# One hybrid-attention layer on one core: the compressed branch's bias table by DMA, its last logits by two products, and transpositions that begin with the selected branch

## The chip, the cores and the metric

The kernel runs on one core of a Trainium2 chip. The core has a matrix engine (TensorE, PE in the rows, with PEld for its weight loads), VectorE (DVE), ScalarE (ACT), GpSimd (POOL) and SyncE (SP), each with an instruction queue of its own that is worked in order. DMAs are started from SP's and POOL's queues, a few from ACT's. The metric is the device time of one execution in microseconds (us), the median of the runs shown.

## The reference

One layer, sequence 512, width 2048, everything in float32:

```
h  = x @ W_in                              (2048 x 11808: q, k, v, gates, z of both attentions)
yA = (FoX(qA, kA, vA, f) * silu(zA)) @ W_A      8 heads of 128, forget-gate bias
yB = (NSA(qB, K/V per branch, gates) * silu(zB)) @ W_B   8 heads, 2 key/value groups
x  = LayerNorm(alpha * x + (sigmoid(gA) * yA + sigmoid(gB) * yB) @ W_o)
```

NSA adds three branches per head, each with its own softmax and its own gate:

```
compressed: 31 blocks of 32 tokens, stride 16; keys/values from a small MLP over each block
            logits = q . k_cmp / sqrt(128) + rel_bias[bucket(t - block_end)], masked where block_end > t
selected:   8 of 8 blocks of 64 tokens at this length, that is causal attention over all 512
window:     the last 512 tokens, causal
every logit gets rel_bias[bucket(distance)] of its head (32 buckets)
```

## The kernel before, in words

Every product of the reference is made in float32 accuracy from split operands: `split` writes a value's rounded part (hi) with ACT and the rest (lo) with DVE, and `mm3` (L106) adds hi x hi, hi x lo and lo x hi into one PSUM bank. A weight tile of 128x512 takes one ACT operation (wh) and one DVE operation (wl) before TensorE can use it.

The program is one long stream of *units*, each of some 12 or more dense products on one weight chunk. Chunks come by SP's queue into three buffers (wr), the splits run three units ahead. Within a unit a *step* of the background work (`tick`) follows every two k-tiles, that is every six dense products. A step advances the generators in `active` and `copies`, then one step of the queue of transposition jobs, then one of the queue of logits jobs. So the order of the instructions on every engine is written out by this program; nothing is decided on the chip, and each engine waits on semaphores in that order.

The stages: first the transposition of x and the first projections, in which `tables` builds the bias tables; then projections by a seven-product scheme with sums on DVE and accumulating DMAs from POOL's queue; the eight FoX heads (about 560 to 840 us), the compression MLP among them (`cmp_units`, `cmp_finish`); the eight NSA heads (about 840 to 1120 us); the outputs.

The bias of the compressed branch: `tables` writes the bias by distance into a row of DRAM (rel_d), `spread` writes it 31 times to DRAM (fwd_d), and in FoX `block_bias` fetches for each head a tile cbT [31 blocks x 512 tokens], whose four 128-token pieces TensorE transposes (L706) into a pt bank, and DVE copies them into cb [128 tokens, head, row tile, 32 blocks]. `nsa_s` adds cb to the compressed logits (L544).

An NSA head has two jobs. `nsa_s` (logits) makes eight items in eight steps: row tiles 0 to 2 of the selected branch together with the compressed one ("sc"), the compressed logits of row tile 3 alone ("c", three products of 32 columns), the selected row tile 3, then three of the window branch. Each item goes through a product, a row minimum and exponential one step later, and a scaling by 1/sum and gate another step later. At step n = 7 the compressed weights are normalised into tc3. `nsa_t` (transpositions and values) waits for the whole of that, then transposes tc3 (L599), the four column tiles of the selected weights p (L417) and those of the window, splits each on ACT and DVE (pT), and three steps after its transposition multiplies it with the values into one bank o. There are two pt banks, two s banks for logits, and one o bank.

Of the kernel before, what the change touches and what calls it, by code (L numbers as in the profile page):

```python
# [40 lines left out]
NEG = -1e30  # L41
SC = DH ** -0.5
RL = 640
FL = 1023
OFF = [P * i * (i + 1) // 2 for i in range(NT)]
PW = P * NT * (NT + 1) // 2
FIRST = 16512
# [16 lines left out]
def layer(ctx, tc, x, w_in, b_f, pos_k, pos_v, wk1, wk2, wv1, wv2, w_a, w_b, w_o, ln_g, ln_b, rel, onehot, out):  # L64
# [446 lines left out]
    def nsa_s(h, st):  # L511
        key, g = ("n", h), h // HPG
        yield from wait_for(("q", key), ("k", ("s", g)), ("k", ("w", g)))
        bt = pool("nsa").tile([P, S], F32, name="bt", tag="bt", bufs=2)
        nc.gpsimd.dma_start(bt, dram(skew_d, h * P * RL + P - 1, [[RL - 1, P], [1, S]]))
        yield
        st["s"], st["st"] = yield from take_p()
        st["w"], st["wt"] = yield from take_p()
        q, k = qt[key], kt_[g]
        tcm = pool("nsa").tile([P, NT, CP], F32, name="tc", tag="tc", bufs=1)  # L520

        def mm(it):
            i, br = it["i"], it["br"]
            n = (i + 1) * P
            t0 = slice(i * P, (i + 1) * P)
            b = bank("s", 2)
            it["bias"] = bt[:, (NT - 1 - i) * P:]
            if i == 0:
                def both(u):
                    return k[:, u, :2 * S].rearrange("p (b c) -> p b c", b=2)[:, :, :CP + P]  # L530
                mm3(b[:, :2 * (CP + P)].rearrange("p (b c) -> p b c", b=2), (q[:, 0, t0], q[:, 1, t0]),
                    (both(0), both(1)), True, True)
                it["b"], it["logits"] = b, b[:, CP:CP + P]
                it["other"].update(logits=b[:, 2 * CP + P:2 * (CP + P)], bias=it["bias"])
                return
            c0 = {"c": 0, "sc": 0, "s": CP, "w": CP + S}[br]
            nn = {"c": CP, "sc": CP + n, "s": n, "w": n}[br]
            mm3(b[:, :nn], (q[:, 0, t0], q[:, 1, t0]), (k[:, 0, c0:c0 + nn], k[:, 1, c0:c0 + nn]), True, True)
            it["b"] = b
            it["logits"] = b[:, CP:CP + n] if br == "sc" else b[:, :n]  # L540

        def red(it):
            if it["br"] in ("c", "sc"):
                nc.vector.tensor_tensor(tcm[:, it["i"]], it["b"][:, :CP], cb[:, h, it["i"]], op=ALU.add)  # L544
            if it["br"] != "c":
                exp_row(it)
# [13 lines left out]

        steps = items("s", 1, [(0, "sc"), (1, "sc"), (2, "sc"), (3, "c"), (3, "s")])
        other = items("w", 2, [(i, "w") for i in range(NT)])
        steps[0]["other"] = other[0]
        steps += other[1:]
        mc, lc, rc = stat("mn"), stat("l"), stat("r")
        for n, _ in enumerate(staged(steps, (mm, red, norm))):
            if n == 5:
                nc.vector.tensor_reduce(mc, tcm, axis=AX.X, op=ALU.max)
                nc.vector.tensor_tensor(tcm, tcm, mc[:, :, None].to_broadcast([P, NT, CP]), op=ALU.subtract)
                nc.scalar.activation(tcm, tcm, AF.Exp)  # L570
            if n == 7:
                nc.vector.tensor_reduce(lc, tcm, axis=AX.X, op=ALU.add)
                nc.vector.reciprocal(rc, lc)
                nc.vector.tensor_tensor(rc, rc, gates[:, :, 3 * h], op=ALU.mult)
                yield from take_later("tc")

                st["c"] = tc3 = pool("nsa").tile([P, NT, C3], F32, name="tc3", tag="tc3", bufs=1)
                nc.vector.tensor_tensor(tc3.rearrange("p i (u c) -> p i u c", u=3),
                                        tcm[:, :, None, :].to_broadcast([P, NT, 3, CP]),
                                        rc[:, :, None, None].to_broadcast([P, NT, 3, CP]), op=ALU.mult)  # L580
            if n == 7:
                done.add(("s", key))
                free["q"] += 1
            yield
        done.add(("p", key))

    def nsa_t(h, st):
        key, g = ("n", h), h // HPG
        yield from wait_for(("p", key), ("v", ("s", g)), ("v", ("w", g)))
        yield from take_later("o")  # L590
        o = bank("o", 1)

        def tr(it):
            if "p" in it:
                tr_p(it)
                return
            it["b"] = b = bank("pt", 2)
            for i in range(NT):
                nc.tensor.transpose(b[:C3, i * P:(i + 1) * P], st["c"][:, i], ident)  # L599
            free["tc"] += 1  # L600

        def spl(it):
            if "p" in it:
                split_p(it)
                return
            it["t"] = t = pt_tile()
            src, c, low = it.pop("b")[:C3], t[:C3, 0], slice(CP, 2 * CP)
            nc.scalar.activation(c, src, AF.Copy)
            nc.vector.tensor_tensor(c[low], src[low], c[low].bitcast(F32), op=ALU.subtract)

        def prod(it):
            if "p" in it:
                pv(it)
                return
            nc.tensor.matmul(o, vt["c", g], it.pop("t")[:C3, 0], start=True, stop=False)

        def items(nm):
            return [dict(j=j, p=st[nm], tag=st[nm + "t"], v=vt[nm, g], o=o, first=False, last=nm == "w" and j == NT - 1)
                    for j in range(NT)]

        yield from staged([{}] + items("s") + items("w"), (tr, spl, None, prod))
        gate_out(key, H + h, o)
        done.add(("t", key))

# [8 lines left out]
        return pool("hd").tile([P, S], F32R, name=name, tag="om", bufs=KT)[:p, :n]  # L633


    rel_d = dp.tile([H, RL + FL], F32, name="rel_d")
    skew_t = dp.tile([H, P, RL], F32, name="skew_d")
    skew_d = skew_t[:]
    fwd_t = dp.tile([H, NCMP, FL], F32, name="fwd_d")
    fwd_d = fwd_t[:]  # L640
    negc_t = dp.tile([H, S], F32, name="negc_d")
    negc_d = negc_t[:]
    zd = [dp.tile([P, S], F32, name=f"z_d{h}") for h in range(NZD)]
# [6 lines left out]
    def tables():  # L650
# [3 lines left out]
        nc.gpsimd.dma_start(po[CMP_LEN:], pos_v[0])  # L654
        neg = small("neg", H, S)
        nc.vector.memset(neg, NEG)
        nc.gpsimd.dma_start(rel_d[:, S:2 * S], neg)
        nc.gpsimd.dma_start(rel_d[:, 2 * S:RL + S - 1], neg[:, :RL - S - 1])
# [10 lines left out]
        for oh, r in zip(ohs, ohr):  # L669
            nc.scalar.activation(r, oh, AF.Copy)  # L670
            yield
        for oh, at in zip(ohr, (0, RL + S - 1)):
# [3 lines left out]
            tb = small("tb", H, S)  # L676
            nc.scalar.activation(tb, m[:H], AF.Copy)
            nc.gpsimd.dma_start(rel_d[:, at:at + S], tb)
# [6 lines left out]

    def spread():

        for t, off, rows_, n in ((skew_d, 0, P, RL), (fwd_d, RL, NCMP, FL)):
            for h in range(H):
                nc.gpsimd.dma_start(t[h], dram(rel_d[:], h * (RL + FL) + off, [[0, rows_], [1, n]]))  # L690
                for _ in range(3):
                    yield

    def block_bias():

        for _ in range(24):
            yield
        for h in range(H):
            t = small("cbT", CP, S)
            nc.gpsimd.memset(t, NEG)  # L700
            nc.gpsimd.dma_start(t[:NCMP], dram(fwd_d, h * NCMP * FL + 480, [[FL - CMP_STRIDE, NCMP], [1, S]]))
            for _ in range(8):
                yield
            m = bank("pt", 2)
            for i in range(NT):
                nc.tensor.transpose(m[:, i * CP:(i + 1) * CP], t[:, i * P:(i + 1) * P], ident[:CP, :CP])  # L706
            nc.vector.tensor_copy(cb[:, h], m[:, :NT * CP].rearrange("p (i c) -> p i c", c=CP))
            yield


    def evac_fg(p):
# [146 lines left out]
    def cmp_finish(kv):  # L858
# [2 lines left out]
        parts = small("parts", 2 * n, CMP_HID)  # L861
        two = small("two", 2 * n, n)
        nc.vector.tensor_copy(parts, hid[kv][:2 * n, :CMP_HID])
        nc.vector.tensor_tensor(two, ident[:2 * n, :n], ident[:2 * n, n:2 * n], op=ALU.add)
        for _ in range(4):
            yield
        m = bank("m", 1)
# [340 lines left out]
    def attention_open():  # L1208
# [5 lines left out]
        open_pool("fox")  # L1214
        active.append(biases())
        active.append(raw_load())
        active.append(block_bias())

    at = {}
    for h in range(H):  # L1220
# [474 lines left out]
```

## Time and profile before

| | |
|---|---|
| median of 3 runs | 1492.75 us (1492.39 to 1493.81) |
| profiled execution | 1492.17 us, its span 1490.0 us |
| TensorE busy | 1477.0 us, 99% of the span |
| DVE busy | 878.1 us, 59% |
| ACT busy | 670.4 us, 45% |
| POOL busy | 236.0 us, 16% |
| granted TensorE clock | 0.998 over the span, the level of 2.4 GHz |

The span is the profiled part of the execution, from its first to its last instruction; the difference to its own time is 2.2 us. A product's recorded busy time holds its passage through the array and overlaps its neighbour's, so that what one costs in a stream is read from start to start. The name before the arrow is the tile written, those behind it are read: `d<-xs,wh` is a dense product, `s<-nk,q` NSA logits, `pt<-ident,p` a transposition of weights, `o<-pT,nvs` and `o<-pT,nvw` the products with the selected and the window values.

### The profile page before, as it was taken

The page shows a single profiled execution, that of the slowest core. Times are in us where ns is not written, and L with a number is a line of the kernel's source. Part 1 is how long each engine was busy: PE and PEld are TensorE (multiplying, and loading weights), DVE is VectorE, ACT ScalarE, POOL GpSimd, SP SyncE. Part 2 cuts the span into 40 slices and gives each one's busy share as a digit, 9 for nine tenths or more (in the row PEclk, how much of TensorE's full clock was granted, in tenths as well). Part 3 has the DMA queues.
Part 4 walks back from the last instruction along what each step waited for, and adds up shares of the span by engine and source line. Part 5 has one row for each costly group of instructions (what it writes and reads, how often), then busy time and mean ns, then how long its engine had stood idle before and what let it go on. Part 6 is the DMA issues. An engine that isn't in the chain of part 4 may idle for free.

```text
span 1490.0 us, 19352 instructions
## 1 busy us (share of the span) xinstructions
PE 1477.0 (99%) x6905; PEld 1219.3 (82%) x6905; DVE 878.1 (59%) x1705; ACT 670.4 (45%) x1284; POOL 236.0 (16%) x375
## 2 busy tenths in 40 slices
PE   8999999999999999999999999999999999999998
PEld 6788888888888888888888888888888888888886
DVE  4666766666666764765664467646675444444445
ACT  6255656565656564544543344434453322322233
POOL 1211130102010206645400000000000100120001
PEclk9999999999999999999999999999999999999999
DMA  8678696868686856553533332232233523362336
GB/s 231 158 222 199 187 187 199 194 190 197 182 205 186 202 142 195 154 162 115 151 112 91 107 79 72 57 107 78 79 99 100 170 92 127 127 227 93 127 113 169
DMA packets 190703, 219.05 MB, mean 147 GB/s; under 512 B 13344, under 2 KB 125008, under 8 KB 190608
## 3 DMA queue, kind: packets, MB, share of 16 engines
q1 hardware_dynamic: 164720, 160.98, 35.7%
q0 software_dynamic: 25600, 56.32, 17.5%
q8 instruction: 54, 0.88, 0.2%
q10 hardware_dynamic: 288, 0.52, 0.1%
q14 instruction: 41, 0.34, 0.1%
HBM read 199.11 MB, written 22.32 MB: 149 GB/s over the span
## 4 chain that ended last, share of the span: by engine, by line
PE 97%; DVE 2%; ACT 1%; issue 0%; DMA 0%; SPq 0%; ACTq 0%
PE d L106 47%; PE s L106 17%; PE o L106 10%; PE pt L106 10%; PE m L106 8%; PE pt L417 2%; PE m L112 1%; PE o L112 1%; PE d L1298 0%; DVE wl L98 0%; ACT p L399 0%; DVE xs L98 0%; DVE p L397 0%; DMA wr<-in_w_in_dram 0%; PE s L1599 0%
## 5 line engine op out<-in xcount | busy, mean ns | idle before, releaser
L98 DVE TENSOR_TENSOR wl<-wr,wh 128x512 fp32r<-128x512 f32 x460 | 317.1, 695 | 289.9 <-ACT wh L97 285.3
L97 ACT ACTIVATE wh<-wr 128x512 fp32r<-128x512 f32 x460 | 286.3, 628 | 361.5 <-PE d L106 113.7
L106 PE MATMUL d<-xs,wh 128*128 128x512 f32 x1376 | 437.3, 399 | 0.5 <-ACT xs L97 0.2
L106 PEld LDWEIGHTS d<-xs,wh 128*128 128x128 f32 x1376 | 248.2, 189 | 47.5 <-DVE xs L98 1.6
L106 PE MATMUL d<-xs,wl 128*128 128x512 f32 x688 | 269.9, 392 | 0.0
L106 PEld LDWEIGHTS d<-xs,wl 128*128 128x128 f32 x688 | 129.5, 188 | 29.0 <-DVE wl L98 0.5
L98 DVE TENSOR_TENSOR wl<-s,wh 128x512 fp32r<-128x512 f32 x144 | 99.6, 693 | 68.7 <-ACT wh L97 66.8
L97 ACT ACTIVATE wh<-s 128x512 fp32r<-128x512 f32 x144 | 91.0, 632 | 82.3 <-DVE wl L98 68.4
L106 PE MATMUL s<-wh,T 128*128 128x512 f32 x384 | 120.2, 389 | 0.0
L399 ACT ACTIVATE p<-p,mn 128x128 f32<-128x128 f32 (+3 forms) x96 | 54.0, 562 | 137.4 <-DVE mn L397 137.4
L106 PE MATMUL d<-wh,xs 128*128 128x512 f32 x336 | 111.2, 391 | 0.0
L106 PE MATMUL m<-wh,xs 128*128 128x512 f32 x256 | 99.7, 390 | 0.0
L106 PE MATMUL o<-wh,xs 128*128 128x512 f32 x240 | 93.5, 389 | 0.0
L106 PEld LDWEIGHTS s<-wh,T 128*128 128x128 f32 x384 | 72.1, 188 | 14.9
L106 PE MATMUL s<-wl,T 128*128 128x512 f32 x192 | 74.7, 389 | 0.0
L106 PEld LDWEIGHTS d<-wh,xs 128*128 128x128 f32 x336 | 63.1, 188 | 12.8
L1029 POOL DMA_DIRECT2D r<-in_w_in_dram x28 | 33.7, 1275 | 225.5 <-ACT zo L1175 176.8
L98 DVE TENSOR_TENSOR pT<-pt,pT 128x512 fp32r<-128x512 f32 (+1 forms) x96 | 46.7, 487 | 38.3 <-ACT pT L97 38.2
L106 PE MATMUL d<-wl,xs 128*128 128x512 f32 x168 | 65.4, 389 | 0.0
L844 POOL TENSOR_SCALAR af<-raw,posT 128x31 f32<-128x31 f32 x128 | 65.0, 528 | 0.6
L97 ACT ACTIVATE pT<-pt 128x512 fp32r<-128x512 f32 (+1 forms) x96 | 41.3, 431 | 45.9 <-PE pt L417 44.7
L106 PE MATMUL pt<-wh,T 128*128 128x512 f32 x192 | 60.1, 389 | 0.0
(334 smaller groups left out, 2484.3 us busy)
## 6 DMA issues: line engine op xcount, KB each, us to landing
wr<-in_w_in_dram SPq DMA_DIRECT2D x147, 512.0 KB, 3.9
wr<-in_w_o_dram SPq DMA_DIRECT2D x32, 512.0 KB, 3.8
r<-in_w_in_dram SPq DMA_DIRECT2D x20, 512.0 KB, 4.7
r<-in_w_in_dram POOLq DMA_DIRECT2D x20, 512.0 KB, 11.2
s<-in_w_in_dram POOLq DMA_DIRECT2D x20, 512.0 KB, 6.3
wr<-in_w_a_dram SPq DMA_DIRECT2D x16, 512.0 KB, 3.7
wr<-in_w_b_dram SPq DMA_DIRECT2D x16, 512.0 KB, 3.7
wr<-in_w_in_dram SPq DMA_DIRECT2D x26, 256.0 KB, 3.6
```

The source lines that it names most:

```text
L97: nc.scalar.activation(hi, src, AF.Copy)
L98: nc.vector.tensor_tensor(lo, src, hi.bitcast(F32), op=ALU.subtract)
L106: nc.tensor.matmul(o, u, v, start=first and n == 0, stop=last and n == 2, **kw)
L112: nc.tensor.matmul(*u, start=first and u is whole, stop=last and u is whole)
L399: nc.scalar.activation(row, row, AF.Exp, bias=it["mn"][:, i:i + 1], scale=-1.0, accum_out=it["l"][:, i:i + 1])
L417: nc.tensor.transpose(b[:, (i - j) * P:(i - j + 1) * P], pt[:, OFF[i] + j * P:OFF[i] + (j + 1) * P], ident)
L844: nc.gpsimd.tensor_scalar(af[:, l, g], src, posT[:, po0 + ll:po0 + ll + 1], None, op0=ALU.add)
L1029: nc.gpsimd.dma_start(st[n][:, k - 1:k + 1, part], src, accum_op=ALU.add)
```

## The change

Four things. (1) The table cb is no longer transposed by TensorE. `tables` lays the bias by distance out as fw [8 heads, 8 residues, 62 multiples of 16], filled with -1e30 where the block lies ahead, sixteen small DMAs write fwd_d [head, 128 tokens, 55], and eight DMAs fetch cb from it in runs of 31 values. `block_bias` goes. (2) The compressed logits of row tile 3 take two products: q hi with k hi and k lo side by side (64 columns), then q lo with k hi onto the first 32; DVE adds both halves. (3) `nsa_t` waits for "ps" alone, which `nsa_s` sets at step 7 (6 in the last head), and transposes the selected branch first, then tc3, then the window. (4) The 0/1 matrix `two`, which adds the halves in `cmp_finish`, is made by POOL instead of DVE.

```
-            c0 = {"c": 0, "sc": 0, "s": CP, "w": CP + S}[br]
-            nn = {"c": CP, "sc": CP + n, "s": n, "w": n}[br]
+            if br == "c":
+                nc.tensor.matmul(b[:, :2 * CP].rearrange("p (u c) -> p u c", u=2), q[:, 0, t0], k[:, :, :CP],
+                                 start=True, stop=False)
+                nc.tensor.matmul(b[:, :CP], q[:, 1, t0], k[:, 0, :CP], start=False, stop=True)
+                it["b"] = b
+                return
+            c0 = {"sc": 0, "s": CP, "w": CP + S}[br]
+            nn = {"sc": CP + n, "s": n, "w": n}[br]
...
+            if it["br"] == "c":
+                nc.vector.tensor_tensor(tcm[:, it["i"]], it["b"][:, CP:2 * CP], tcm[:, it["i"]], op=ALU.add)
...
+            if n == (7 if h < H - 1 else 6):
+                done.add(("ps", key))
...
-        yield from wait_for(("p", key), ("v", ("s", g)), ("v", ("w", g)))
+        yield from wait_for(("ps", key), ("v", ("s", g)), ("v", ("w", g)))
...
-        yield from staged([{}] + items("s") + items("w"), (tr, spl, None, prod))
+        yield from staged(items("s") + [{}] + items("w"), (tr, spl, None, prod))
...
+        RH = CMP_STRIDE // 2
+        fw = [small("fw", H, RH * FM) for _ in range(2)]
+        for t in fw:
+            nc.vector.memset(t, NEG)
...
+            for u, t in enumerate(fw):
+                tv = t.rearrange("h (r m) -> h r m", m=FM)
+                nc.scalar.activation(tv[:, :, m0:], mv[:, u * RH:(u + 1) * RH], AF.Copy)
...
+            for a in range(P // CMP_STRIDE):
+                for u, t in enumerate(fw):
+                    r0 = a * CMP_STRIDE + u * RH
+                    nc.gpsimd.dma_start(fwd_d[:, r0:r0 + RH], t.rearrange("h (r m) -> h r m", m=FM)[:, :, a:a + FW])
+                yield
...
-        for t, off, rows_, n in ((skew_d, 0, P, RL), (fwd_d, RL, NCMP, FL)):
...
+        for h in range(H):
+            src = dram(fwd_d[:], h * P * FW, [[FW, P], [P // CMP_STRIDE, NT], [1, NCMP]])
+            nc.gpsimd.dma_start(cb[:, h, :, :NCMP], src)
+            for _ in range(3):
+                yield
-    def block_bias():
...
-        nc.vector.tensor_tensor(two, ident[:2 * n, :n], ident[:2 * n, n:2 * n], op=ALU.add)
+        nc.gpsimd.memset(two, 0.0)
+        for v in range(G + 1):
+            nc.gpsimd.affine_select(two, two, pattern=[[1, n]], compare_op=ALU.not_equal, fill=1.0,
+                                    base=1 - (2 * v + 1) * NCMP, channel_multiplier=1)
...
-        active.append(block_bias())
```

TensorE in a FoX head, around the first transpositions of cbT (v is the head's values), in the program before:

```order
L106 MATMUL d<-xs,wh 128x512 x2
L106 MATMUL d<-xs,wl 128x512
L706 MATMUL pt<-ident,cbT 128x32 x4
L106 MATMUL o<-pT,v 128x128 x3
L106 MATMUL d<-xs,wh 128x512 x2
L106 MATMUL d<-xs,wl 128x512
L106 MATMUL d<-xs,wh 128x512 x2
```

And in the changed program (its `mm3` is L107, one line further down):

```order
L107 MATMUL d<-xs,wh 128x512 x2
L107 MATMUL d<-xs,wl 128x512
L107 MATMUL o<-pT,v 128x128 x3
L107 MATMUL d<-xs,wh 128x512 x2
L107 MATMUL d<-xs,wl 128x512
L107 MATMUL d<-xs,wh 128x512 x2
```

The four transpositions are gone, and the value products follow the dense ones directly; the same holds for the other seven places.

TensorE at the start of head 0's transpositions in NSA (p the weights, tc those of the compressed branch, nk the keys of the group, s the logits bank), before. The head's last logits stand twelve rows of dense products ahead of this piece:

```order
L106 MATMUL d<-xs,wh 128x512 x2
L106 MATMUL d<-xs,wl 128x512
L106 MATMUL d<-xs,wh 128x512 x2
L106 MATMUL d<-xs,wl 128x512
L599 MATMUL pt<-ident,tc_8128 96x128 x4
L106 MATMUL d<-xs,wh 128x512 x2
L106 MATMUL d<-xs,wl 128x512
L106 MATMUL d<-xs,wh 128x512 x2
L106 MATMUL d<-xs,wl 128x512
L417 MATMUL pt<-ident,p 128x128 x4
L106 MATMUL s<-nk,q 128x320 x3
```

In the changed program, from the head's last logits on:

```order
L107 MATMUL s<-nk,q 128x512 x3
L107 MATMUL d<-xs,wh 128x512 x2
L107 MATMUL d<-xs,wl 128x512
L107 MATMUL d<-xs,wh 128x512 x2
L107 MATMUL d<-xs,wl 128x512
L418 MATMUL pt<-ident,p 128x128 x4
L107 MATMUL d<-xs,wh 128x512 x2
L107 MATMUL d<-xs,wl 128x512
L107 MATMUL d<-xs,wh 128x512 x2
L107 MATMUL d<-xs,wl 128x512
L418 MATMUL pt<-ident,p 128x128 x3
```

The transposition of p follows one step of dense products behind the last logits. Before, tc came first, four steps behind them, and p one step later; logits of head 1 followed p directly, and now they don't.

POOL's DMAs in the first stages (rel_d the bias by distance, skew_d the table of the other two branches, r and s the sums of the next stage), before:

```order
L678 DMA rel_d<-tb 8x512 x2
L690 DMA skew_d<-rel_d 128x640 x2
L733 AFFINE_SELECT gates<-gates 128x8
L690 DMA skew_d<-rel_d 128x640
L755 MEMSET fone 8x512
L690 DMA skew_d<-rel_d 128x640
L762 DMA negc_d<-fsum 8x512
L690 DMA skew_d<-rel_d 128x640 x4
L690 DMA fwd_d<-rel_d 31x1023 x8
L1029 DMA r<-in_w_in_dram 128x2x512 x4
L1029 DMA s<-in_w_in_dram 128x2x512 x4
```

And now:

```order
L696 DMA rel_d<-tb 8x512
L712 DMA fwd_d<-fw 8x8x55 x10
L756 AFFINE_SELECT gates<-gates 128x8
L712 DMA fwd_d<-fw 8x8x55 x6
L778 MEMSET fone 8x512
L723 DMA skew_d<-rel_d 128x640
L785 DMA negc_d<-fsum 8x512
L723 DMA skew_d<-rel_d 128x640 x7
L729 DMA cb<-fwd_d 128x4x31 x8
L1056 DMA r<-in_w_in_dram 128x2x512 x4
L1056 DMA s<-in_w_in_dram 128x2x512 x4
```

Sixteen small writes of fwd_d go ahead of the skew_d writes, and eight loads of cb stand where the eight writes of fwd_d were.

## Rows read from the trace of the kernel before

**Rows 1.** The page: busy time by engine, and the chain that ended last.
```profile
PE 1477.0 (99%) x6905; PEld 1219.3 (82%) x6905; DVE 878.1 (59%) x1705; ACT 670.4 (45%) x1284; POOL 236.0 (16%) x375
...
PE 97%; DVE 2%; ACT 1%; issue 0%; DMA 0%; SPq 0%; ACTq 0%
```

**Rows 2.** Waits of TensorE: waiting line, waited for, us, times, longest.
```profile
PE s L1599 <- DMA xa<-in_x_dram: 4.5, 1, 4.5
PE pt L417 <- DVE pT L98: 0.6, 1, 0.6
PE s L106 <- DVE mn L397: 0.5, 1, 0.5
PE d L106 <- DVE xs L98: 0.4, 2, 0.2
...
PE pt L706 <- issue: 0.2, 1, 0.2
```

**Rows 3.** Groups of TensorE's instructions by form: count, busy us, mean ns.
```profile
L106 PE MATMUL s<-nk,q 128*128 128x32 f32 x24 | 3.7, 255 | 0.0
...
L706 PE MATMUL pt<-ident,cbT 32*128 32x32 f32 x32 | 3.4, 226 | 0.2 <-issue 0.2
```

**Rows 4.** TensorE's timeline around one passage of cbT: start us, busy us.
```profile
622.34 0.40 PE L106 MATMUL d<-xs,wl 128*128 128x512 f32 x1
622.58 0.62 PE L106 MATMUL d<-xs,wh 128*128 128x512 f32 x2
623.03 0.39 PE L106 MATMUL d<-xs,wl 128*128 128x512 f32 x1
623.35 0.43 PE L706 MATMUL pt<-ident,cbT 32*128 32x32 f32 x4
623.71 0.74 PE L106 MATMUL d<-xs,wh 128*128 128x512 f32 x2
624.29 0.40 PE L106 MATMUL d<-xs,wl 128*128 128x512 f32 x1
```

**Rows 5.** Tile cb: ns min/median/max of one, first and last start us.
```profile
L544 DVE TENSOR_TENSOR tc<-s,cb x32: 172/184/191, 861.7 to 1110.8; 128x32 f32<-128x32 f32 x32
L707 DVE COPY cb<-pt x8: 277/288/292, 609.4 to 718.7; 128x128 f32<-128x128 f32 x8
```

**Rows 6.** POOL's timeline between the first two stages; idle before, in brackets.
```profile
78.47 0.51 POOL L690 DMA_DIRECT2D fwd_d<-rel_d  x1 [2.56 <-DMA skew_d<-rel_d]
103.84 1.28 POOL L1029 DMA_DIRECT2D r<-in_w_in_dram  x1 [24.86 <-DVE wl L98]
```

**Rows 7.** POOL's timeline in FoX, near the compression's end.
```profile
656.70 1.68 POOL L507 TENSOR_SCALAR_AFFINE_SELECT cbx<-cbr 128x128 f32<-128x128 f32 x4 [5.20 <-DVE mn L397]
```

**Rows 8.** TensorE's timeline around head 0's compressed logits of row tile 3.
```profile
865.74 0.39 PE L106 MATMUL d<-xs,wl 128*128 128x512 f32 x1
865.97 0.40 PE L106 MATMUL s<-nk,q 128*128 128x32 f32 x3
866.22 0.71 PE L106 MATMUL d<-xs,wh 128*128 128x512 f32 x2
866.77 0.40 PE L106 MATMUL d<-xs,wl 128*128 128x512 f32 x1
```

**Rows 9.** TensorE's timeline in the last head.
```profile
1108.30 0.95 PE L106 MATMUL s<-nk,q 128*128 128x512 f32 x3 [0.52 <-DVE mn L397]
```

**Rows 10.** Timeline of head 0: the last selected row scaled, the last logits.
```profile
870.92 0.55 DVE L406 TENSOR_SCALAR p<-p,r,gates 128x512 f32<-128x512 f32 x1
...
873.39 0.85 PE L106 MATMUL s<-nk,q 128*128 128x512 f32 x3
```

**Rows 11.** DMA issues, 10 to 30 us: KB each, us to landing.
```profile
fgr<-in_w_in_dram SPq DMA_DIRECT2D x1, 192.0 KB, 7.2
```

**Rows 12.** DMA issues over the span.
```profile
wr<-in_w_in_dram SPq DMA_DIRECT2D x147, 512.0 KB, 3.9
```

More of the change, by code (lines that the diff above doesn't have):

```diff
@@ L43 @@
 RL = 640
-FL = 1023
+FM = S // CMP_STRIDE + NCMP - 1
+FW = FM - P // CMP_STRIDE + 1
 OFF = [P * i * (i + 1) // 2 for i in range(NT)]
@@ L614, in prod @@
                 return
-            nc.tensor.matmul(o, vt["c", g], it.pop("t")[:C3, 0], start=True, stop=False)
+            nc.tensor.matmul(o, vt["c", g], it.pop("t")[:C3, 0], start=False, stop=False)
         def items(nm):
-            return [dict(j=j, p=st[nm], tag=st[nm + "t"], v=vt[nm, g], o=o, first=False, last=nm == "w" and j == NT - 1)
+            return [dict(j=j, p=st[nm], tag=st[nm + "t"], v=vt[nm, g], o=o, first=nm == "s" and j == 0,
+                         last=nm == "w" and j == NT - 1)
                     for j in range(NT)]
-        yield from staged([{}] + items("s") + items("w"), (tr, spl, None, prod))
+        yield from staged(items("s") + [{}] + items("w"), (tr, spl, None, prod))
         gate_out(key, H + h, o)
@@ L633, in small_r @@
         return pool("hd").tile([P, S], F32R, name=name, tag="om", bufs=KT)[:p, :n]
-    rel_d = dp.tile([H, RL + FL], F32, name="rel_d")
+    rel_d = dp.tile([H, RL], F32, name="rel_d")
     skew_t = dp.tile([H, P, RL], F32, name="skew_d")
     skew_d = skew_t[:]
-    fwd_t = dp.tile([H, NCMP, FL], F32, name="fwd_d")
-    fwd_d = fwd_t[:]
+    fwd_d = dp.tile([H, P, FW], F32, name="fwd_d")
     negc_t = dp.tile([H, S], F32, name="negc_d")
@@ L656, in tables @@
         nc.vector.memset(neg, NEG)
-        nc.gpsimd.dma_start(rel_d[:, S:2 * S], neg)
-        nc.gpsimd.dma_start(rel_d[:, 2 * S:RL + S - 1], neg[:, :RL - S - 1])
+        nc.gpsimd.dma_start(rel_d[:, S:], neg[:, :RL - S])
+        nc.gpsimd.memset(cb[:, :, :, NCMP:], NEG)
         ohs = [small("oh", BUCKETS, S) for _ in range(2)]
@@ L671, in tables @@
             yield
-        for oh, at in zip(ohr, (0, RL + S - 1)):
+        RH = CMP_STRIDE // 2
+        fw = [small("fw", H, RH * FM) for _ in range(2)]
+        for t in fw:
+            nc.vector.memset(t, NEG)
+        for n, oh in enumerate(ohr):
             m = bank("m", 1)
@@ L675, in tables @@
                 nc.tensor.matmul(m[:H], rbs[:, u * H:(u + 1) * H], oh, start=u == 0, stop=u == 1)
-            tb = small("tb", H, S)
-            nc.scalar.activation(tb, m[:H], AF.Copy)
-            nc.gpsimd.dma_start(rel_d[:, at:at + S], tb)
-            yield
+            if n == 0:
+                tb = small("tb", H, S)
+                nc.scalar.activation(tb, m[:H], AF.Copy)
+                nc.gpsimd.dma_start(rel_d[:, :S], tb)
+                yield
+                continue
+            m0 = FM - NCMP + 1
+            mv = m[:H, 1:1 + (FM - m0) * CMP_STRIDE].rearrange("h (m r) -> h r m", r=CMP_STRIDE)
+            for u, t in enumerate(fw):
+                tv = t.rearrange("h (r m) -> h r m", m=FM)
+                nc.scalar.activation(tv[:, :, m0:], mv[:, u * RH:(u + 1) * RH], AF.Copy)
+                if u:
+                    nc.scalar.activation(tv[:, RH - 1, m0 - 1:m0], m[:H, :1], AF.Copy)
+            yield
+            for a in range(P // CMP_STRIDE):
[3 more added lines that the diff above has]
+                yield
         copies.append(spread())
@@ L686, in spread @@
     def spread():
-        for t, off, rows_, n in ((skew_d, 0, P, RL), (fwd_d, RL, NCMP, FL)):
[L689 to L692, printed above, removed]
-    def block_bias():
-        for _ in range(24):
-            yield
         for h in range(H):
[L699 to L702, printed above, removed]
+            nc.gpsimd.dma_start(skew_d[h], dram(rel_d[:], h * RL, [[0, P], [1, RL]]))
+            for _ in range(3):
                 yield
[L704 to L708, printed above, removed]
+        for h in range(H):
+            src = dram(fwd_d[:], h * P * FW, [[FW, P], [P // CMP_STRIDE, NT], [1, NCMP]])
+            nc.gpsimd.dma_start(cb[:, h, :, :NCMP], src)
+            for _ in range(3):
+                yield
     def evac_fg(p):
```

## The prediction

> **What bounds the kernel now.** I read the page first. TensorE is busy for 99% of the span, and of the chain that ended last 97% is TensorE's own time [rows 1]: the program is one stream of products, and what is taken out of that stream is gained unless another engine is late in its place. So the waits come second: in the list of what TensorE waited for, apart from 4.5 us for the first tile of x at the start, no entry is over 0.6 us: 0.6 on DVE's split of a transposed tile, 0.5 on DVE's row minimum (mn), 0.4 on weight splits (xs), 0.2 at the block-bias transpositions [rows 2]. That leaves three questions: what the removed products take in the stream, what the new order of the attention steps adds, and which of the small waits grows once TensorE comes earlier. For the first I read TensorE's timeline where such a piece stands among 128x512 products, and count from start to start, since the busy times of products overlap.
>
> **The change part by part.**
>
> *Block bias.* The 32 transpositions of cbT [rows 3] and the 8 copies behind them go. One passage of four: the last wl product before it starts at 623.03 and the next wh product at 623.71, that is 0.68 us, where the same step without a passage (622.34 to 622.58) takes 0.24: 0.44 for the passage. The pair after it is late too, since its weights could not be loaded ahead: from 623.71 to 624.29 is 0.58 us against 0.45 (622.58 to 623.03): 0.13 more [rows 4]. Together 0.57 us, eight times: 4.6 us. The 0.2 us wait before one passage [rows 2] goes with it. DVE loses 8 x 0.29 us of copies [rows 5], which are off the path. Ends: 3.5 us (without the late pair, 8 x 0.44) and 4.8.
>
> *What builds the table instead.* Two fw tiles are filled by DVE and ACT in the first stage, sixteen small DMAs write fwd_d, eight DMAs fetch cb with runs of 124 B. cb is first read by head 0 of NSA (the trace reads it from 861.7 us on), so only what stands in the way counts. On POOL's queue the new DMAs take the place of the eight fwd_d ones of before, whose last was issued at 78.47; the next that POOL issues, r<-in_w_in, came 24.86 us of idling later, at 103.84, released by DVE [rows 6]. I cost it at nothing; the cover is those 25 us, and without it every us more would push the accumulating loads of the next stage. The sum matrix "two" moves from one DVE operation to a memset and three selects on POOL. The nearest row is four selects of up to 128x512 in 1.68 us, before which POOL idled 5.20 us [rows 7]. Nothing again, with the four program steps up to its product as cover; if POOL were late by the whole of it, 2 x 1.7 us.
>
> *Two products, not three.* Per head the last row tile's compressed logits were three products of 32 columns [rows 3], and become one of 64 and one of 32. In head 0 the three take from 865.97 to 866.22, 0.25 us, 0.08 each [rows 8]. I take one of them away, 8 x 0.08 = 0.7 us, and give the 32 further columns no price, because each of these small products takes much the same step whatever its width: four transpositions of 32 columns took 0.36 us, 0.09 each [rows 4]. Ends: nothing (64 columns cost as two of 32) and 1.0 us (half of the 0.25 goes). The second addition on DVE costs 0.18 us a head [rows 5], beside TensorE's work.
>
> *The earlier start.* No product goes or comes. Head 0 opens its transpositions one program step after its last logits, where the old order had four; the tc transpositions follow the selected branch. Counted in the order of TensorE's instructions, the attention work stands in 125 separate places among the dense products, and before in 115. A place costs the late pair behind it: 866.22 to 866.77 is 0.55 us where 0.45 is usual, 0.10 [rows 8, 4]. Ten more make 1.0 us at most; separate pieces lose changes of width inside a place, so I take 0.5 us. Ends: 0 and 1.0.
>
> *Who becomes late.* In the FoX stage TensorE comes 0.57 us earlier after every passage, while DVE's chain gets only its 0.29 us copy shorter. Where TensorE already waits for DVE there (0.6 us on pT [rows 2]) part of the gain comes back: two or three places of 0.3 us, 0.6 us taken, ends 0 and 1.5. In the last NSA head and the fill behind it, the 0.5 us on mn (0.52 idle at 1108.30 [rows 9]) and the 0.4 on xs [rows 2] come from DVE doing the transposed tiles of head 6, the rows of head 7 and the splits of FoX outputs at once. With transpositions three steps earlier the first of these is mostly gone before the rows of head 7 begin. I take 0.5 us of gain; ends: 0.9 gained, 1.0 lost.
>
> *Sum.* 4.6 + 0.2 + 0.7 = 5.5 out; 0.5 + 0.6 come back; 0.5 more out: 4.9 us. The profiled execution took 1492.17 us (span 1490.0, 2.2 around it), so 1487.3. The median of the runs is 0.58 above that execution: 1487.9.
>
> **The rivals.**
>
> *The gain is swallowed.* TensorE, early, waits for DVE and ACT, whose chains in FoX and in the logits phases set the pace. For it: the waits on DVE in [rows 2], and 59% of busy time on DVE [rows 1], unevenly spread. Against it: those waits are 1.5 us in all. It would need 2 us and more to come back, doubling the FoX waits and turning the tail's gain into a loss: 5.5 - 1.0 - 1.5 - 1.0 = 2.0, so 1490.8. A page would put the time near there by another way. The Trainium skill, page "TensorE: Matmul & The Clock Gate", section "Back-to-back issue gap", gives a product of 1 to 64 columns about 25 ns from start to start. By that rule the 40 removed products are worth 1.0 us as an estimate, and the sum would be near no change. The trace does not agree: 0.09 us each in the passage, and the late pair besides [rows 4].
>
> *The wait moves on to the transpositions: slower.* TensorE works in order; if the selected rows are not normalised when it reaches the first transposition, everything behind stands, the dense products first. In head 0 the last selected row was scaled by DVE from 870.92 to 871.47, and the last logits product started at 873.39 [rows 10]; the transposition stands behind these three products and six dense ones, so not before 873.39 + 9 x 0.23 = 875.5. The slack is 4.0 us. For it: in the last head the opening comes one step sooner yet, and there TensorE already waits for DVE [rows 9]. Against it: DVE would have to be later by over 4 us in most heads. From 1.0 us of waiting per head (8 against the 4.9 gained and 3.0 of the bound below) it decides; with 1.2 us a head, 9.6 us lost, the time is 1497.5.
>
> *Small runs hold up the weights.* The eight cb loads are 4096 runs of 124 B. The nearest row is a load of 192 KB in 2048 runs of 96 B, which took 7.2 us to land [rows 11]; two of these are 14.4 us. Weight chunks land in 3.9 us [rows 12], three buffers stand ready, and each feeds 24 products of 0.23 us, 5.5 us; if the chunks were held for the whole 14.4, TensorE would lose 14.4 - 11.0 = 3.4 us: 1491.3. Against it: the fwd_d loads that go were in the same place. The Trainium skill, page "DMA: Bandwidth & Descriptors", section "Specifications", asks for 512 B or more per transfer for line rate, which speaks for this rival and not for its size. The 7.2 us for a mere 192 KB agree with that rule.
>
> **How the numbers follow.** My forecast, with gains between 3 and 7.5 us, has 0.76. The swallowed gain 0.16, the small runs 0.04, the late transpositions 0.04. What a measurement can tell from no change is 0.2%, 3.0 us, so the line lies at 1489.8. The forecast's own range is 1485.8 to 1489.7: at its foot everything stands at its better end (4.8 + 1.0 + 0.9 + 0.2, nothing back: 6.9 of gain), at its head the FoX waits and the places at their worse ends. To leave out no more than 2 in 10 it reaches into the swallowed gain, and a little under the foot for the scatter of the runs: 1485.3 to 1490.8. Faster: 0.78, the forecast and a little of the second case. Slower: 0.05, the late transpositions and a little of the small runs. The rest, 0.17, is within the bound.
>
> **What would show it.** Right: 40 products fewer; between 600 and 760 us the TensorE stream is about 4 us shorter; each head's last-tile passage has two small products; waits of TensorE after 600 us add up to no more than 3 us, with the one on mn smaller or gone; the weights' landing between 60 and 105 us as before. Wrong: a wait of pt<-ident,p on p (late rows), a longer wait on pT, a or z in FoX, a wait of r<-in_w_in on cb or fwd_d, or a product with "two" that waits for POOL. If the NSA stage itself is longer by more than 1 us with no wait shown, the price of the places is wrong.

## The result, and the profile after

The changed kernel takes 1501.01 us (median of 6 runs, 1499.58 to 1501.68); the kernel before took 1492.72 beside it (6 runs). The ratio is 1.0054, with a 95% interval of 1.0043 to 1.0065: slower by 8 us, where 4.9 us less was forecast. The profiled execution took 1499.73 us, its span 1498.0.

The page of the changed kernel, busy time by engine, and the engines' shares of the chain that ended last:

```profile
PE 1472.3 (98%) x6865; PEld 1214.8 (81%) x6865; DVE 879.1 (59%) x1705; ACT 671.6 (45%) x1286; POOL 241.9 (16%) x382
...
PE 91%; DVE 5%; ACT 2%; issue 1%; DMA 0%; SPq 0%; ACTq 0%; DVEq 0%
```

TensorE does 4.7 us less work than in [rows 1], as the removed products should give, and the span is 8.0 us longer. Of the chain 91% is TensorE's own instead of 97%; the shares of DVE and ACT have grown from 2% and 1% to 5% and 2%. What TensorE waited for (waiting line, releaser, us, times, longest; tc are the compressed logits, mn a row's minimum, a an operand of the compression MLP, z the output gate of a FoX head):

```profile
PE pt L418 <- DVE pT L99: 10.5, 10, 1.6
PE s L1625 <- DMA xa<-in_x_dram: 4.4, 1, 4.4
PE s L107 <- DVE tc L554: 1.2, 1, 1.2
PE s L107 <- DVE mn L398: 0.9, 1, 0.9
PE m L113 <- DVE a L99: 0.7, 1, 0.7
PE pt L418 <- DVE z L302: 0.4, 1, 0.4
```

The first row was 0.6 us and one time in [rows 2]; now it is 10.5 us and ten times. These rows without the load of x make 13.7 us; in the old list pT, mn, z, a and the one before cbT made 1.8 (0.6, 0.5, 0.3, 0.2, 0.2), of which [rows 2] leaves these two out:

```profile
PE pt L417 <- DVE z L301: 0.3, 1, 0.3
...
PE m L112 <- DVE a L98: 0.2, 1, 0.2
```

So 11.9 us of waiting came and 4.7 us of work went, 7.2 of the 8.0 us. The places are to be seen in TensorE's timeline (start us, busy us, and idle before in brackets), one in FoX, one in each NSA head and a second one in the last head. Shown are FoX, heads 0 and 4 and the last; the other heads waited 0.67, 0.35, 1.03, 1.06 and 0.51 us:

```profile
631.70 0.44 PE L418 MATMUL pt<-ident,p 128*128 128x128 f32 x2 [1.35 <-DVE pT L99]
...
877.73 0.44 PE L418 MATMUL pt<-ident,p 128*128 128x128 f32 x2 [1.61 <-DVE pT L99]
...
1023.83 0.44 PE L418 MATMUL pt<-ident,p 128*128 128x128 f32 x2 [1.64 <-DVE pT L99]
...
1126.35 0.44 PE L418 MATMUL pt<-ident,p 128*128 128x128 f32 x2 [1.04 <-DVE pT L99]
1130.10 0.33 PE L418 MATMUL pt<-ident,p 128*128 128x128 f32 x1 [1.26 <-DVE pT L99]
```

In every head it is the row of two pieces, the third column tile: the first that needs a pt bank which another transposition of this head has filled. In the last head the fourth waits too. Head 0 of the changed kernel, PE, DVE and ACT side by side, shows what holds that bank:

```profile
868.25 0.55 DVE L407 TENSOR_SCALAR p<-p,r,gates 128x512 f32<-128x512 f32 x1
...
870.33 0.85 PE L107 MATMUL s<-nk,q 128*128 128x512 f32 x3
...
872.38 0.60 PE L418 MATMUL pt<-ident,p 128*128 128x128 f32 x4
...
874.23 0.49 PE L418 MATMUL pt<-ident,p 128*128 128x128 f32 x3
874.28 0.68 DVE L398 CUSTOM_DVE_ANT_0 p<-s,bt 128x512 f32<-128x512 f32 x1
...
875.01 0.72 ACT L400 ACTIVATE p<-p,mn 128x512 f32<-128x512 f32 x1 [1.69 <-DVE mn L398]
...
875.73 0.62 ACT L98 ACTIVATE wh<-wr 128x512 fp32r<-128x512 f32 x1
876.25 0.95 ACT L98 ACTIVATE pT<-pt 128x512 fp32r<-128x512 f32 x2
876.38 0.69 DVE L99 TENSOR_TENSOR wl<-wr,wh 128x512 fp32r<-128x512 f32 x1 [1.41 <-ACT wh L98]
876.99 0.68 DVE L99 TENSOR_TENSOR pT<-pt,pT 128x512 fp32r<-128x512 f32 x1
...
877.73 0.44 PE L418 MATMUL pt<-ident,p 128*128 128x128 f32 x2 [1.61 <-DVE pT L99]
```

The last logits products start 3.1 us earlier than in [rows 10] (870.33 against 873.39), so the gain of the other parts is there when the heads begin. The first tile is transposed by 873.0, with no wait: the last selected row was scaled by 868.8. But its copy to pT on ACT begins only at 876.25 and DVE's half ends at 877.7. In between ACT and DVE finish, in the order of their queues, the last row of the window branch: its reduction on DVE (874.28), its exponential on ACT (875.01), a weight split. ACT was idle for 1.69 us ahead of that exponential, with the first tile ready in its bank: it stood in line, it was not busy. The second tile took the other pt bank at 874.23, so the third stands until 877.73, and everything behind it on TensorE with it.

In the last head two logits products wait besides:

```profile
1113.72 0.94 PE L107 MATMUL s<-nk,q 128*128 128x512 f32 x3 [0.90 <-DVE mn L398]
...
1117.22 0.59 PE L107 MATMUL s<-nk,q 128*128 128x256 f32 x3 [1.19 <-DVE tc L554]
```

The first is the wait of [rows 9], grown from 0.52 to 0.90; the second is new.

### The profile page after: what moved, and what is told of

Same layout as the page of the kernel before. It is cut to its first block, busy times and chain, and to the rows that moved or that the text cites. A ratio compares the mean times of both kernels' runs of the same rounds, so it can differ in the third digit from the quotient of the medians.

```text
span 1498.0 us, 19280 instructions
## 1 busy us (share of the span) xinstructions
PE 1472.3 (98%) x6865; PEld 1214.8 (81%) x6865; DVE 879.1 (59%) x1705; ACT 671.6 (45%) x1286; POOL 241.9 (16%) x382
## 4 chain that ended last, share of the span: by engine, by line
PE 91%; DVE 5%; ACT 2%; issue 1%; DMA 0%; SPq 0%; ACTq 0%; DVEq 0%
PE d L107 43%; PE s L107 16%; PE o L107 10%; PE pt L107 10%; PE m L107 8%; PE pt L418 2%; DVE wl L99 2%; DVE p L398 1%; ACT p L400 1%; PE m L113 1%; ACT wh L98 1%; DVE p L407 1%; PE o L113 0%; DVE pT L99 0%; PE d L1324 0%
## 5 line engine op out<-in xcount | busy, mean ns | idle before, releaser
L107 PE MATMUL d<-xs,wh 128*128 128x512 f32 x1376 | 438.0, 399 | 0.5 <-ACT xs L98 0.2
L107 PEld LDWEIGHTS d<-xs,wh 128*128 128x128 f32 x1376 | 247.2, 189 | 46.7 <-DVE xs L99 1.6
L107 PE MATMUL d<-xs,wl 128*128 128x512 f32 x688 | 270.2, 393 | 0.3 <-DVE wl L99 0.2
L107 PEld LDWEIGHTS d<-xs,wl 128*128 128x128 f32 x688 | 129.3, 188 | 30.1 <-DVE wl L99 1.8
L107 PE MATMUL s<-wh,T 128*128 128x512 f32 x384 | 120.2, 389 | 0.0
L107 PE MATMUL d<-wh,xs 128*128 128x512 f32 x336 | 111.4, 391 | 0.0
L107 PE MATMUL m<-wh,xs 128*128 128x512 f32 x256 | 99.7, 389 | 0.0
L107 PE MATMUL o<-wh,xs 128*128 128x512 f32 x240 | 93.4, 389 | 0.0
L107 PEld LDWEIGHTS s<-wh,T 128*128 128x128 f32 x384 | 72.1, 188 | 15.0
L107 PE MATMUL s<-wl,T 128*128 128x512 f32 x192 | 74.7, 389 | 0.0
L107 PEld LDWEIGHTS d<-wh,xs 128*128 128x128 f32 x336 | 63.1, 188 | 12.9
L107 PE MATMUL d<-wl,xs 128*128 128x512 f32 x168 | 65.4, 389 | 0.0
L107 PE MATMUL pt<-wh,T 128*128 128x512 f32 x192 | 60.1, 389 | 0.0
## 6 DMA issues: line engine op xcount, KB each, us to landing
r<-in_w_in_dram POOLq DMA_DIRECT2D x20, 512.0 KB, 11.5
```

The source lines that it names most:

```text
L107: nc.tensor.matmul(o, u, v, start=first and n == 0, stop=last and n == 2, **kw)
```

## The experiments

Each kernel was timed in five rounds beside the kernel before on the same chip; what compares is the ratio. The last column is TensorE's waiting for a transposition's bank or weights in heads 0 to 6 (862 to 1100 us). "Opened at p" means that a head's transpositions wait for all its rows, as in the kernel before, and "split at once" that a tile is copied out of its bank in the step of its transposition and not one step later.

| kernel | median, us | ratio to before (95%) | waits, us (times) |
|---|---|---|---|
| changed | 1501.01 | 1.0054 (1.0043 to 1.0065) | 6.9 (7) |
| e1 old transpositions, other parts | 1489.41 | 0.9977 (0.9968 to 0.9986) | none |
| e2 new transpositions alone | 1501.91 | 1.0060 (1.0048 to 1.0073) | 5.4 (6) |
| e3 selected first, opened at p | 1490.88 | 0.9985 (0.9976 to 0.9994) | none |
| e4 first tile split at once | 1497.12 | 1.0025 (1.0015 to 1.0036) | 2.6 (5) |
| e5 opened one step later | 1498.87 | 1.0041 (1.0028 to 1.0053) | 3.6 (5) |
| e6 opened two steps later | 1493.41 | 1.0005 (0.9996 to 1.0014) | 0.3 (2) |
| e7 two tiles split at once | 1491.31 | 0.9990 (0.9981 to 0.9999) | none |
| e8 early, compressed first | 1501.14 | 1.0053 (1.0040 to 1.0066) | 4.8 (6) |
| e9 e1, splits at once in FoX | 1487.63 | 0.9966 (0.9952 to 0.9980) | none |
| e10 early in the last head only | 1493.31 | 1.0004 (0.9995 to 1.0012) | none |
| e11 e7, last head opened at p | 1489.93 | 0.9982 (0.9973 to 0.9990) | none |

**e1**: the changed kernel with the old opening and order.

```
-            if n == (7 if h < H - 1 else 6):
-                done.add(("ps", key))
...
-        yield from wait_for(("ps", key), ("v", ("s", g)), ("v", ("w", g)))
+        yield from wait_for(("p", key), ("v", ("s", g)), ("v", ("w", g)))
...
-        yield from staged(items("s") + [{}] + items("w"), (tr, spl, None, prod))
+        yield from staged([{}] + items("s") + items("w"), (tr, spl, None, prod))
```

> The changed kernel with the transpositions of NSA as before: opening after the last row's scaling (p), compressed branch first. The table by DMA, the two products and the sum matrix on POOL stay. Theory Q (queue position: the new waits of TensorE in the eight heads and the last head come from the early opening, where the split of the first transposed tile stands behind the window rows in ACT's and DVE's queues): the 2.9 us that TensorE was ahead at NSA's start stay, 0.1 us per head from the two products come on top, so 1492.7 - 3.6 = 1489.1, from 1488.3 to 1490.3. Rival D (the other parts cost time that the trace does not show as a wait, the small-run DMAs for one): over 1493.

Measured 1489.41, 4.1 us under its runs of before by the medians, 3.4 by the ratio. Between 862 and 1140 us only small waits of the last head are left, 0.2 us on a weight split and these two:

```profile
PE s L107 <- DVE mn L398: 0.6, 1, 0.6
PE s L107 <- DVE tc L554: 0.4, 1, 0.4
```

Parts 1, 2 and 4 together make the kernel faster; rival D is out.

**e2**: the reverse, the two edits above put into the kernel before.

> The kernel before with the new transpositions alone: opened three steps sooner, four in the last head, selected branch first. Theory Q: the 11.3 us that the changed kernel lost from the start of NSA on, without the gain of the other parts: 1492.7 + 11.3 = 1504.0, from 1501.5 to 1506. Rival D: at most 1495.

Measured 1501.91, in Q's range at its lower end, 8.4 us over its before by the medians and 9.0 by the ratio, with the waits on the same row of two pieces in six of heads 0 to 6:

```profile
PE pt L417 <- DVE pT L98: 5.4, 6, 1.2
```

So the new transpositions carry the loss alone. They cost 9.0 us here and 11.5 in the changed kernel (its ratio against e1's): the heads' waits are 1.5 us shorter here. Why they are was not tested.

**e3** keeps the new order and undoes only the opening (the first two pieces of e1's diff).

> The changed kernel, selected branch first, but opened only when all rows are scaled (p), as before. Theory Q: no wait of a transposition on pT in the NSA heads; 1489.3, from 1488.3 to 1491. Rival O (the order costs, since the compressed branch now stands in the middle of the group and its split delays the window's): a good part of the 11 us stays, 1495 to 1501.

Measured 1490.88, in Q's range: no wait in heads 0 to 6. The order is not what costs; rival O is out. The intervals of e3 and e1 overlap. Of the 2.2 us between their profiled executions 1.8 was there before FoX, 1.5 of it within the first 30 us, where both programs do the same.

**e8** is the fourth corner: the new opening (step 7 in all heads) with the old order.

> The other corner: opened three steps sooner in all eight heads, but the compressed branch first, as before, then selected and window. Theory Q: the bank of the compressed branch's tile is given back behind the last window row just so, and the second selected transposition waits for it: 1499, from 1496.5 to 1502. Rival O (the loss needs the new order): at most 1492.

Measured 1501.14, in Q's range, but not at Q's place, so that its size came out by luck:

```profile
PE pt L611 <- DVE tc L588: 4.2, 5, 1.3
PE pt L418 <- DVE pT L621: 0.6, 1, 0.6
```

With the compressed branch first, TensorE waits for the compressed weights themselves, whose scaling by 1/sum DVE ends late; the bank of that tile makes only 0.6 us. Rival O is out: early is the cause in both orders; what it waits for depends on what comes first.

**e4** opens as early as the changed kernel, and puts one pair of instructions forward: the split of the first tile.

```
             if "p" in it:
                 tr_p(it)
+                if it["first"]:
+                    split_p(it)
                 return
...
             if "p" in it:
-                split_p(it)
+                if not it["first"]:
+                    split_p(it)
                 return
```

> The changed kernel, opened early as in it, but the first transposed tile of each head is split by ACT and DVE in the step of its transposition, not one step later, so that in both queues its split stands ahead of the last window row's reduction and exponential. Theory Q: the wait of the third transposition goes in heads 0 to 6 (8.1 us) and mostly in head 7 (1.2 of 2.6 us); the two waits of head 7's logits (2.4 us) stay: 1501.0 - 9.3 = 1491.7, from 1490 to 1494. Rival T (throughput: DVE and ACT have too much to do in this stretch, whatever the order): the wait moves to the fourth transposition or to the value products, 1498 to 1502.

Measured 1497.12, between the ranges of Q and T: 4 us back, not 9.3. Head 0 of this kernel:

```profile
876.13 0.69 DVE L99 TENSOR_TENSOR pT<-pt,pT 128x512 fp32r<-128x512 f32 x1
...
878.25 0.38 PE L418 MATMUL pt<-ident,p 128*128 128x128 f32 x2
...
880.22 0.55 DVE L407 TENSOR_SCALAR p<-p,r,gates 128x512 f32<-128x512 f32 x1
880.68 0.55 DVE L99 TENSOR_TENSOR pT<-pt,pT 128x384 fp32r<-128x384 f32 x1
...
881.29 0.33 PE L418 MATMUL pt<-ident,p 128*128 128x128 f32 x1 [0.58 <-DVE pT L99]
```

The first tile's split is done before the third transposition, which has no wait any more. The second tile's split still stands behind the last window row (its scaling at 880.22), and now the fourth transposition waits, 2.6 us in five heads, and the last head's 2.5. That is part of rival T's picture, moved rather than gone. The next kernel tells whether it is throughput.

**e7**: the second tile too (`now = nm == "s" and j < 2` in place of `first`).

> As the kernel whose first transposed tile is split in the step of its transposition, and the second tile too. Theory Q: there the wait moved to the fourth transposition (0.74, 0.64, 0.75, 0.65, 0.64 us in five heads, 2.6 in the last), which waits for the second tile's split, still behind the last window row; now that goes too: 1497.1 - 3.4 - 1 = 1492.7, from 1491 to 1495. Rival T: the work that is put ahead makes the window rows late, and the wait moves to the next bank or to the weights' splits: 1496 to 1500.

Measured 1491.31, in Q's range, and in heads 0 to 6 no wait of TensorE at all, with the opening as early as in the changed kernel and the same work on DVE and ACT. In these heads it was the position in the queues, not the throughput of the two engines. Left over are the last head's 2.1 us on logits and 1.4 on the compressed tile's bank.

**e5 and e6** open one and two steps later: `n == (8 if h < H - 1 else 7)` and `(9 ... else 8)`.

> The changed kernel, opened one step later in every head (step 8, in the last head 7). Theory Q (queue position): one step is six dense products, 1.36 us, by which TensorE comes later to the third transposition, while the rows of the window branch end where they did; of the waits 1.79, 0.84, 0.52, 1.20, 1.81, 1.24, 0.68 in heads 0 to 6 some 0.9 us is left, and the last head's 2.6 us halve: 1501.0 - 8.5 = 1492.5, from 1490.5 to 1494.5. Rival T (throughput: DVE and ACT cannot do the transposed tiles any faster in this stretch): the waits stay, over 1497.

> The changed kernel, opened two steps later in every head (step 9, in the last head 8). Theory Q: no wait of a transposition on pT in heads 0 to 6, the last head as with the opening at p (1.7 us on its logits, none or little on its transpositions): 1490.5, from 1489 to 1492. Rival T: over 1495.

Both missed. The time of e5 even lies where rival T put it, but T's waits did not stay. In heads 0 to 6 the waits fall from 6.9 to 3.6 and to 0.3 us, but one step buys less than its 1.36 us, since the split moves too. In e5 it stands behind the next piece of the same row, its scaling:

```profile
876.84 0.55 DVE L407 TENSOR_SCALAR p<-p,r,gates 128x512 f32<-128x512 f32 x1
...
877.30 0.69 DVE L99 TENSOR_TENSOR pT<-pt,pT 128x512 fp32r<-128x512 f32 x1
...
878.04 0.44 PE L418 MATMUL pt<-ident,p 128*128 128x128 f32 x2 [0.91 <-DVE pT L99]
```

And the last head does not wait less on its bank: 3.4 us in e5 and 2.3 in e6, where the changed kernel has 2.3. Splits of the last weights stand in the same queues there; whether they are the reason was not tested.

**e10**: opening at p in heads 0 to 6, at step 6 in the last head alone.

> Selected branch first, opened at p in heads 0 to 6, and four steps sooner in the last head alone. Theory Q: the last head's two waits of a transposition (1.2 and 1.4 us in the changed kernel) and nothing else beside the kernel opened at p everywhere: 1490.9 + 2.6 = 1493.5, from 1492 to 1495. Rival L (the last head gains from its early opening, since less is left for the end, and the loss is in heads 0 to 6 only): 1489 to 1490.5.

Measured 1493.31, by the ratios 2.8 us over e3, which differs in the last head alone. That is in Q's range, though as one wait of 3.2 us on a bank and not as two of 1.2 and 1.4. The early opening gains nothing in the last head either; rival L is out. The logits' waits of the last head (1.0 us on mn and 0.5 on tc) are as in e3.

**e11**: e7, with the last head opened at p.

> Two tiles split at once, opened three steps sooner in heads 0 to 6, and at p in the last. Theory Q: the last head's wait for the compressed tile's bank (1.5 us) goes, its logits' waits (2.4 us) shrink to the 1.75 us of the kernel opened at p: 1491.3 - 2.2 = 1489.1, from 1487.8 to 1490.8. Rival G (the early opening in heads 0 to 6 gains something of its own once nothing waits): under 1487.8. Rival T: over 1490.8.

Measured 1489.93, in Q's range. The wait on the bank is gone, the logits' waits are not shorter: 1.2 us on tc and 0.9 on mn. The one on tc is 0.9 to 1.2 us in every kernel whose head 6 opens three steps sooner and 0.4 or 0.5 where head 6 opens at p (e1, e3, e9, e10), so it belongs to head 6's opening. The one on mn doesn't: it is 1.0 in e3 and e10 too. With no wait in heads 0 to 6 the early opening still gains nothing over e1 (0.9982 against 0.9977): rival G is out.

**e9** carries the cure to FoX: e1, the first tile and z split in the step of their transposition.

```
             if "p" in it:
                 tr_p(it)
+                if it["j"] == 0:
+                    split_p(it)
                 return
...
+            silu2(zt[key], it.pop("b"))
...
-            if "p" in it:
+            if "p" in it and it["j"]:
                 split_p(it)
-            else:
-                silu2(zt[key], it.pop("b"))
```

> The kernel with the old NSA transpositions (1489.4, faster than before), and in the FoX heads the first transposed tile and z split in the step of their transposition. Theory Q carried to FoX: the two waits of a transposition that are left there (1.5 us on pT near 630 us, 0.6 on z near 723 us) are of the same kind, a bank given back late because its split is queued behind other work, and go: 1489.4 - 2.1 = 1487.3, from 1486 to 1489. Rival W: the split that goes ahead makes the weights' splits late, TensorE waits for these instead: 1489.4 or more.

Measured 1487.63, the lowest of all and 0.34% under before, in Q's range. Neither of the two waits is left in its profile, while the ten other profiled kernels with the new FoX stage all have both, 0.4 to 1.4 us on pT and 0.4 or 1.6 on z. So the waits are of the kind that Q said, and the wait on weight splits in FoX stays at 0.2 us, as in e1: nothing of rival W. That it beats the kernel before and the changed one is shown; that it beats e1 is not. The intervals overlap, the two profiled executions are alike (1488.40 and 1488.66 us), and though TensorE gained 4.1 us on the kernel before between 569 and 770 us, where it gained 2.7 in e1, it gained 4.0 there in e5, whose FoX stage is that of the changed kernel.

## Why the prediction was wrong

The step that failed is in the rival "The wait moves on to the transpositions": it made late rows the only way in which a transposition can wait ("DVE would have to be later by over 4 us in most heads"), so that the sum priced the earlier start by its places alone and put the wait at nothing. It asked the right question, who is late when TensorE gets there, and answered it for one of two things that a transposition needs: the rows that it reads. Their slack was forecast as 4.0 us and was 3.6 in head 0 (scaled by 868.80, transposed from 872.38), and the first transposition never waited. It also needs a free pt bank. There are two, the third transposition is two steps behind the first, and its bank comes free only when ACT and DVE have copied the first tile. In the old order that copy stood behind all rows of the head; opened three steps sooner, it stands among them. I looked at the ready time of the data and not at the place of the *following* operation in the queues of the engines that drain the bank. The rival had 0.04 and a price of 9.6 us for eight heads; by e1 the price was 11.5 us. That the two are near is luck: no row was late, the wait of 0.35 to 1.64 us a head was for the bank, and the last head and its logits came on top.

*Block bias.* Right: 4.6 + 0.2 forecast, 4.7 measured. Both programs have the same dense products in the same order, so each step from one to the next can be compared. Around seven of the eight passages TensorE is 0.55 or 0.56 us faster, and 0.78 at the one that had waited. The first passage, before and then in the changed kernel:

```profile
608.61 0.39 PE L106 MATMUL d<-xs,wl 128*128 128x512 f32 x1
608.93 0.43 PE L706 MATMUL pt<-ident,cbT 32*128 32x32 f32 x4
609.29 0.55 PE L106 MATMUL o<-pT,v 128*128 128x128 f32 x3
609.68 0.68 PE L106 MATMUL d<-xs,wh 128*128 128x512 f32 x2
```

```profile
608.40 0.40 PE L107 MATMUL d<-xs,wl 128*128 128x512 f32 x1
608.64 0.45 PE L107 MATMUL o<-pT,v 128*128 128x128 f32 x3
608.92 0.67 PE L107 MATMUL d<-xs,wh 128*128 128x512 f32 x2
```

From wl to wh is 1.07 us before and 0.52 now. In the four places where `o<-pT,v` follows, as here, the pair behind is as late with the transpositions as without, but the passage costs 0.55 or 0.56 (0.78 with the wait) and not 0.44; in the other four it is 0.45 and a late pair of 0.10 or 0.11. So the forecast, read from one passage, came out for all eight.

*Who becomes late in FoX.* Too small: 0.6 us taken, with ends of 0 and 1.5, and 2.1 measured. Between 569 and 770 us TensorE gained 2.6 us on the kernel before, of the 4.7. In waits 1.5 us came back: pT 0.63 to 1.35, a 0.19 to 0.71, z 0.3 to 0.4 and a new one of 0.17 on a weight split. The rest is spread over steps that grew by 0.15 us or less. The kind was foreseen, "a longer wait on pT, a or z" is among the signs of being wrong; the size was not.

*What builds the table.* Right. On POOL of the changed kernel the last cb load and the next issue stand like this:

```profile
79.05 0.75 POOL L729 DMA_DIRECT2D cb<-fwd_d  x1 [0.65 <-DMA skew_d<-rel_d]
102.75 1.23 POOL L1056 DMA_DIRECT2D r<-in_w_in_dram  x1 [22.95 <-DMA r<-in_w_in_dram]
```

The 25 us of cover [rows 6] are still 23 us. Weight chunks issued between 60 and 110 us landed in 6.4 us, 6.6 before: the rival of the small runs is out, and nothing waited for "two".

*Two products, not three.* 0.7 forecast, 0.9 measured. The passage in head 0 of the changed kernel, for [rows 8]:

```profile
863.05 0.19 PE L539 MATMUL s<-nk,q 128*128 128x64 f32 x1
863.08 0.26 PE L541 MATMUL s<-nk,q 128*128 128x32 f32 x1
863.19 0.71 PE L107 MATMUL d<-xs,wh 128*128 128x512 f32 x2
```

From the first small product to the next wh is 0.14 us, 0.25 before: one step of 0.11 is gone, and the 32 further columns cost nothing, as supposed. Eight times 0.11 is 0.9, and in e1, whose other work stands as before, each of the first seven places is 0.09 to 0.11 us shorter (in the last head's another wait stands beside it).

*The places.* 0.5 us taken, nothing found. The kernel to read this from is e11, which has 126 places, the kernel before 115, and no waits in heads 0 to 6. From the start of NSA to its end it lost 0.5 us on the kernel before, while its waits there grew by 1.6 us (2.3 against 0.7) and the two products saved 0.9.

*The tail.* A gain of 0.5 us was forecast; it became a loss of 3.7: 2.3 us on banks and 2.1 on logits, where 0.7 had been. The sum took it that the tiles of head 6 would be out of the way before the rows of head 7 begin. Instead the wait on mn grew, and head 6's opening added the one on tc.

The predicted sum without the two terms of the early opening, 5.5 - 0.6 = 4.9, stands against e1's 3.4 us by the ratio (2.1 to 4.8) and 4.1 by the medians. So the removed products were priced rightly, and what is missing is what FoX took back: 4.7 + 0.9 - 2.1 = 3.5. One bound of the range is not worked out as it says: with the FoX waits and the places at their worse ends the gain is 5.5 - 1.5 - 1.0 = 3.0 us (1489.7) only if the tail's gain is left out as well. The outcome does not hang on it.

## What to carry to other kernels

Before an operation is moved forward on the engine that bounds the kernel, ask not only whether its inputs are ready but where its output buffer is emptied: take the emptying instruction's new place in the in-order queues of the engines that do it, and what stands ahead of it there. With two buffers, as here, the wait shows two operations later, on an instruction that was not the one moved first. Two cures were tried: a later opening (e3, e6) and an earlier emptying (e7, e11). A third bank was not. And where the bounding engine has hardly any idle time to fill, as here with 99%, ask what an earlier start of one of its jobs can gain at all: without any wait in heads 0 to 6, e7 and e11 are no faster than e1.

## What the runs showed that was not expected

At the end of the wait in e6's last head TensorE fell to its lower level for a while. TensorE's timeline of e6, six products ahead of the wait and six behind it, and then the windows of the wait and of what follows (us; PE, PEld, DVE, ACT and POOL busy, granted clock, DMA share, GB/s):

```profile
1117.63 1.63 PE L107 MATMUL d<-xs 128*128 128x512 f32 x6
...
1122.28 0.69 PE L418 MATMUL pt<-ident,p 128*128 128x128 f32 x2 [2.33 <-DVE pT L99]
1122.62 2.88 PE L107 MATMUL d<-xs 128*128 128x512 f32 x6
```

```profile
1119.50:1122.40 2.90, 0.56 (x3) 0.14 (x3) 2.69 (x6) 2.04 (x5) 0.00 (x0) 0.92 0.24 75
1122.40:1125.30 2.90, 2.90 (x8) 2.35 (x9) 1.31 (x3) 0.38 (x1) 0.00 (x0) 0.50 0.70 223
```

Six products took 2.88 us instead of 1.63, at a granted clock of 0.50, which is the 1.2 GHz level: the wait of 2.3 us cost some 1.3 us more behind it. In e5 the same followed a wait of 3.4 us (0.52 over 3.1 us), and this is part of why both missed their expectations. It did not follow a wait of 3.17 us in the profiled execution of e10, where the granted clock was 1.00:

```profile
1121.90 0.44 PE L418 MATMUL pt<-ident,p 128*128 128x128 f32 x2 [3.17 <-DVE pT L99]
1122.09 1.64 PE L107 MATMUL d<-xs 128*128 128x512 f32 x6
```

Nor did it follow one of 2.5 us in e4's. So the length of the wait alone does not decide it. The same program may do both: the mean granted clock over the span, which is known for every execution, was 0.998 in the profiled one of e10 and 0.996 or 0.997 in five of its eleven, and these five took 1493.3 to 1494.8 us, the six at 0.998 from 1492.1 to 1494.1. (As an estimate, 3 us at 0.50 take 0.001 off the mean over 1490 us.) A profile shows one execution, and what decides stays open.
